# Half of the meta keys on either side of each key strip, their probabilities transposed once per four strips

## The chip, the cores and the metric

The kernel runs on one core of a Trainium2 chip. The metric is the time of one execution on the device in microseconds (us), as the median of several runs. The engines are named as in the profile: PE is TensorE's matrix multiplication, PEld its loading of weights, DVE is VectorE, ACT is ScalarE, POOL is GpSimd, SP is SyncE, which here only issues DMAs.

## The reference, cut to what matters

One layer of an encoder trunk: a combined input projection, a neighbourhood attention over a grid of 16 rows and 64 columns (1024 tokens), a gated linear recurrence, a gated merge, a feed-forward block. The change touches the attention alone. Each of 1024 tokens attends, in each of 8 heads of 64 dimensions, to the tokens of a window of 8 rows and 16 columns around it, and always to 16 learned meta keys; one softmax runs over both.

```
s_win  = einsum(q, k_window) * scale          # + bias, -1e30 outside of the window
s_meta = einsum('bhrcd,bmhd->bhrcm', q, k_meta) * scale       # 16 per token
p      = softmax(concat([s_win, s_meta]))
o      = einsum(p_win, v_window) + einsum('bhrcm,bmhd->brchd', p_meta, v_meta)
```

## The kernel before, in words

**Tiling.** A strip is 8 of the 64 grid columns in all 16 rows, that is 128 tokens; there are 8 strips. A query strip `s` needs the key strips `s-1`, `s` and `s+1` (strips 0 and 7 have two). Heads are worked on in pairs: the loop `for p in range(NPAIR)` (L547) makes four passes, and in each of them the two heads `i` stand on partitions 0 to 63 and 64 to 127 of the projections.

**Numbers in two parts.** Products of fp32 precision are made from a high part (a rounded copy, written by ACT) and a low part (the rest, a DVE subtraction); the helper `split` (L95) does both. `KS`/`KL` hold the high and low parts of the keys, `QX` those of the queries on the two halves of the partitions, `V` the high part in its first 64 columns and the low part in the second 64.

**The keys.** `KS` and `KL` are laid out as 8 strips of `SW = 144` columns: 128 keys of the strip and then all 16 meta keys (L531, L577 to L581). The scores of strip `s` are one product over the neighbouring strips, 432 columns (288 at both ends), so the 16 meta keys come three times in it; the mask `NB` (built from `wmask` on the host, and the bias) lets only those of the centre strip count.

**`scores(s, i)`** (L605): two matmuls (L612, L613), a DVE operation that adds the mask and takes the row's minimum (L618), ACT's exponential with the row sum (L620), the reciprocal and the multiplication by it on DVE (L621, L622). The result is a tile `pr` of 432 columns, five buffers.

**`values(s, i)`** (L625): the probabilities are transposed in blocks of 128 columns on PE, one per key strip (L633) and a fourth one for the centre's meta columns (L635), which takes the 16 meta columns and the 112 before them. All go into one PSUM bank of the tag `t` (two banks) and are split into `PH` and `PL` by ACT (L644) and DVE (L645). Every fourth strip, a group, the products with the values follow into one bank `ov`: one over 512 columns with the meta values in `V[:, 8]` (zero in the rows that aren't meta) for the high parts (L649), two for each of five key strips (L656 high parts, L657 low parts), and one over 512 columns for the low parts of the meta keys (L658). DVE then adds both halves of `ov` into `OT` (L660, L662).

There are 16 steps `(s, i)` in a pass, and the values of a step come two steps behind its scores. A pass has four groups, the kernel 16.

**What sets the order.** The framework's planner draws up the order of each engine's instructions at build time from the dependencies and from the order of the program, as a static list for each engine. It mixes the projections of the next pass (L135 to L137, three matmuls for each of 8 blocks) among the attention of this one; in the last pass the first gate products (L691 to L693) take that part. `block_sums` (L600) makes POOL build sums for a later stage, and POOL adds the bias to the mask (L555). `KS`, `KL`, `QX`, `V` and `NB` have one buffer each, so those of the next pass wait for this one's last reader.

## Time and profile before

| | |
|---|---|
| median of 3 runs | 1551.93 us (1550.94 to 1554.89) |
| the profiled execution | 1550.2 us, its span 1548.4 us |
| PE busy | 1502.1 us, 97% of the span |
| PEld busy | 1253.5 us, 81% |
| DVE busy | 1008.4 us, 65% |
| ACT busy | 654.7 us, 42% |
| POOL busy | 401.8 us, 26% |
| mean granted TensorE clock | 0.998 |

Busy is the share of the span in which an engine worked on at least one instruction. Matmuls overlap, so the duration of a single one is longer than the distance to the next one's start; where a cost on PE is meant, it is the distance between starts that counts.

### The profile page before, as it was taken

The numbers are of one execution on the slowest core, as the hardware profiler recorded it, in microseconds if no ns is written. First come the engines' busy times: TensorE is split into PE (matmuls) and PEld (weight loads), VectorE is DVE, ScalarE is ACT, GpSimd is POOL, SyncE is SP. The second block draws the span as 40 slices with busy tenths as digits, with TensorE's granted clock in tenths as the row PEclk, the third lists the DMA queues.
The fourth block names the chain that finished last, engine by engine and source line by source line (L and its number), as shares of the span: only waits on it lengthen the run. The fifth ranks groups of instructions, "written<-read, shape, count | busy, mean of one in ns | idle before, by whom it ended". The sixth has DMA issues, their size and how long they took to land.

```text
span 1548.4 us, 23448 instructions
## 1 busy us (share of the span) xinstructions
PE 1502.1 (97%) x9188; PEld 1253.5 (81%) x9188; DVE 1008.4 (65%) x1592; ACT 654.7 (42%) x1168; POOL 401.8 (26%) x359
## 2 busy tenths in 40 slices
PE   6999999999999998999999999999999999999998
PEld 5788888878888887888888887888888788887886
DVE  6666666664876877666475369666666444879566
ACT  6231313124665666334122245555555433434444
POOL 4413131315315310011000032444444200237033
PEclk9999999999999999999999999999999999999999
DMA  5101010113123128434951324444444576563224
GB/s 181 43 28 56 28 56 28 55 29 128 49 72 119 55 69 272 136 123 163 339 178 41 109 91 148 165 155 153 153 150 148 169 273 233 190 231 107 98 82 150
DMA packets 142335, 195.61 MB, mean 126 GB/s; under 512 B 8064, under 2 KB 90112, under 8 KB 142224
## 3 DMA queue, kind: packets, MB, share of 16 engines
q1 hardware_dynamic: 133856, 173.40, 33.8%
q10 hardware_dynamic: 6192, 13.37, 2.2%
q0 software_dynamic: 2176, 7.34, 1.3%
q8 instruction: 72, 1.18, 0.3%
q14 instruction: 39, 0.32, 0.1%
HBM read 139.55 MB, written 54.53 MB: 125 GB/s over the span
## 4 chain that ended last, share of the span: by engine, by line
PE 83%; DVE 9%; issue 3%; ACT 2%; DMA 2%; POOL 1%; DVEq 0%; POOLq 0%; SPq 0%; ACTq 0%
PE mm L135 11%; PE mm L136 10%; PE mm L137 10%; PE mm L1112 4%; PE pa L1112 4%; PE pb L691 4%; PE pb L692 4%; PE pb L693 4%; PE pc L1112 4%; PE pb L1112 4%; PE pc L693 2%; PE pc L692 2%; PE pc L691 2%; PE pa L692 2%; PE pa L691 2%
## 5 line engine op out<-in xcount | busy, mean ns | idle before, releaser
L135 PE MATMUL mm<-aT,hi 128*128 128x512 f32 (+2 forms) x640 | 230.2, 360 | 2.7 <-DVE QX L563 1.5
L137 PE MATMUL mm<-aT,lo 128*128 128x512 f32 (+2 forms) x640 | 227.8, 356 | 0.0
L136 PE MATMUL mm<-aT,hi 128*128 128x512 f32 (+2 forms) x640 | 226.6, 354 | 0.0
L97 DVE TENSOR_TENSOR dl<-ur,dh 128x1024 fp32r<-128x1024 f32 x55 | 76.6, 1393 | 93.7 <-ACT dh L96 93.5
L135 PEld LDWEIGHTS mm<-aT,hi 128*128 128x128 f32 x640 | 121.9, 191 | 17.2 <-issue 1.7
L137 PEld LDWEIGHTS mm<-aT,lo 128*128 128x128 f32 x640 | 121.8, 190 | 13.5 <-POOL lo L126 0.3
L136 PEld LDWEIGHTS mm<-aT,hi 128*128 128x128 f32 x640 | 121.9, 190 | 12.4
L96 ACT CAST dh<-ur 128x1024 fp32r<-128x1024 f32 x55 | 57.9, 1053 | 162.5 <-issue 78.1
L125 ACT CAST hi<-raw 128x1024 fp32r<-128x1024 f32 x36 | 37.8, 1051 | 106.7 <-PE mm L136 75.6
L974 ACT CAST wh<-sx 128x512 fp32r<-128x512 f32 x70 | 42.5, 618 | 94.7 <-DMA sx<-in_w_up 33.1
L975 DVE TENSOR_TENSOR wl<-sx,wh 128x512 fp32r<-128x512 f32 x70 | 51.2, 738 | 31.0 <-ACT wh L974 31.0
L975 DVE TENSOR_TENSOR wl<-raw,wh 128x512 fp32r<-128x512 f32 x46 | 50.2, 1090 | 23.7 <-ACT wh L974 22.9
L979 ACT ACTIVATE uv<-uv 128x512 f32<-128x512 f32 x48 | 30.4, 632 | 67.4 <-DVE uv L1090 50.0
L1095 POOL TENSOR_TENSOR us<-u,uv 128x512 f32<-128x512 f32 x15 | 24.0, 1603 | 133.4 <-ACT uv L980 133.4
L1202 POOL TENSOR_TENSOR w<-w,tt 128x512 f32<-128x512 f32 x16 | 23.3, 1458 | 134.0 <-DVE tt L1201 120.4
L399 POOL TENSOR_TENSOR Y<-X,TN 128x512 f32<-128x512 f32 x20 | 35.0, 1749 | 86.1 <-DVE X L396 86.1
L691 PE MATMUL pb<-nt,wh 128*128 128x512 f32 x128 | 50.4, 394 | 3.6 <-DVE uv L1083 2.6
L126 DVE TENSOR_TENSOR lo<-raw,hi 128x1024 fp32r<-128x1024 f32 x34 | 43.2, 1270 | 15.6 <-ACT hi L125 15.4
L92 POOL TENSOR_SCALAR rtm<-ssq 128x1 f32<-128x1 f32 (+1 forms) x17 | 6.4, 376 | 180.4 <-ACT junk L924 156.0
L618 DVE CUSTOM_DVE_ANT_0 pr<-nsc,NB 128x432 f32<-128x432 f32 (+1 forms) x64 | 35.2, 559 | 26.6 <-PE nsc L613 26.5
L1112 PE MATMUL mm<-dl,dh 128*128 128x512 f32 x126 | 49.9, 396 | 2.1 <-DVE dl L97 2.1
L135 PE MATMUL mm<-o,hi 128*128 128x512 f32 x128 | 50.0, 390 | 0.6 <-DVE mix L850 0.6
(380 smaller groups left out, 4409.3 us busy)
## 6 DMA issues: line engine op xcount, KB each, us to landing
raw<-in_w_in SPq DMA_DIRECT2D x56, 512.0 KB, 3.9
ur<-usp SPq DMA_DIRECT2D x55, 512.0 KB, 3.5
raw<-in_w_up SPq DMA_DIRECT2D x16, 1024.0 KB, 5.5
usp<-us SPq DMA_DIRECT2D x60, 256.0 KB, 2.0
sg<-gsp SPq DMA_DIRECT2D x16, 512.0 KB, 4.3
w<-in_w_dn SPq DMA_DIRECT2D x16, 512.0 KB, 4.5
usp<-uv SPq DMA_DIRECT2D x30, 256.0 KB, 2.2
gsp<-gv ACTq DMA_DIRECT2D x24, 256.0 KB, 2.4
```

The lines of the kernel that those rows point to most:

```text
L96: act.copy(hi, src)
L97: dve.tensor_tensor(lo, src, hi.bitcast(F32), op=ALU.subtract)
L126: eng.tensor_tensor(lo[:, :kc], raw[:, :kc], hi[:, :kc].bitcast(F32), op=ALU.subtract)
L135: pe.matmul(ps, lh, rh, start=first, stop=False)
L136: pe.matmul(ps, lh, rl, start=False, stop=False)
L137: pe.matmul(ps, ll, rh, start=False, stop=last)
L691: pe.matmul(ps, lhs[0][:, c], rhs[0][:, k], start=first and k == 0, stop=False, skip_group_check=True)
L692: pe.matmul(ps, lhs[0][:, c], rhs[1][:, k], start=False, stop=False, skip_group_check=True)
L693: pe.matmul(ps, lhs[1][:, c], rhs[0][:, k], start=False, stop=k == 3, skip_group_check=True)
L974: act.copy(v(hi), src)
L975: dve.tensor_tensor(v(lo), src, v(hi).bitcast(F32), op=ALU.subtract)
L1112: pe.matmul(ps, a[n == 2][:, q, j * P:(j + 1) * P], b[n == 1][:, q], start=first and n == 0, stop=last and n == 2, skip_group_check=True)
```

## The change

The meta keys are split into two halves of 8. The key tile becomes one row of 10 blocks of 136 columns, `[8 meta, 128 keys, 8 meta, 128 keys, ...]`, the halves taking turns. The scores of a middle strip are cut out so that the centre's keys have 8 meta keys on either side: 128 + 8 + 128 + 8 + 128 = 400 columns, each meta key once; at both ends 272 columns. Four strips write into one tile `pr` (two buffers). After the fourth, one DVE copy gathers the meta columns of all four into a tile `pm` of 64 columns. `values` transposes three blocks for a strip (two at the ends), and once in a group `pm`; from this, ACT writes the high parts to partitions 0 to 63 of `PM` and DVE the low parts to partitions 64 to 127. The two products over 512 columns are replaced by four over 128 columns, one per strip, with a weight tile `VM` each, in which the meta values stand in that strip's 16 rows twice (against the high and against the low parts). `VM` is made in each pass by four POOL multiplications with a small mask `mmask`, loaded once. A separate transpose and split for the meta values replaces the ninth block of `V`; the meta values are copied by three ACT instructions in place of one.

```
-SW = P + NM
+SW = P + NM // 2
+KO = NM // 2
+KW = 10 * SW
...
-        KS = [npl.tile([P, 8, SW], F32R, name=f"KS{i}") for i in range(2)]
+        KS = [npl.tile([P, KW], F32R, name=f"KS{i}") for i in range(2)]
...
-        V = npr.tile([P, 9, 2, P], F32R, name="Vn")
+        V = npr.tile([P, 8, 2, P], F32R, name="Vn")
+        VM = npr.tile([P, 2, 4, P], F32R, name="VM")
+        mm_sb = npr.tile([P, 2, 4], F32, name="mm_sb")
+        sp.dma_start(mm_sb.rearrange("p a b -> p (a b)"), mmask)
...
             def mev_vn(ps):
-                act.copy(vT[:, 8, P - NM:], ps)
+                v8 = vT[:, 8].rearrange("p (a c) -> p a c", c=2 * NM)
+                for o, m, n in ((0, 0, NM), (NM, KO, KO), (NM + KO, 0, KO)):
+                    act.copy(v8[:, :, o:o + n], ps[:, m:m + n].unsqueeze(1).broadcast_to([P, 4, n]))
...
+            pt = bank("t", "vmt")
+            pe.transpose(pt[:, 0], vT[:, 8], ident)
+            vh = npr.tile([P, P], F32R, tag="vh", name="vh")
+            vl = npr.tile([P, P], F32, tag="vl", name="vl")
+            split(vh, vl, pt[:, 0])
+            for q, v in enumerate((vh.bitcast(F32), vl)):
+                for i in range(2):
+                    pool.tensor_tensor(VM[:, i, :, 64 * q:64 * q + 64],
+                                       v[:, 64 * i:64 * i + 64].unsqueeze(1).broadcast_to([P, 4, 64]),
+                                       mm_sb[:, q].unsqueeze(2).broadcast_to([P, 4, 64]), op=ALU.mult)
...
             def scores(s, i):
-                w = len(js) * SW
+                e = s % 4
+                if e == 0:
+                    po["pr"] = npr.tile([P, 4, 2 * SW + P], F32, tag="pr", name="pr", bufs=2)
+                k0, c0, w, o = ((0, P, 2 * SW, 408) if s == 0 else
+                                (KO + (s - 1) * SW, 0, 2 * SW, 688) if s == 7 else
+                                (KO + (s - 1) * SW, 0, 2 * SW + P, 0))
+                pe.matmul(sc[:, :w], QX[i][:, s], KS[i][:, k0:k0 + w], start=True, stop=False)
+                pe.matmul(sc[:, :w], QX[i][:, s], KL[i][:, k0:k0 + w], start=False, stop=True)
+                prw = pr[:, e, c0:c0 + w]
...
+                if e == 3:
+                    po["pm", i] = npr.tile([P, 8 * KO], F32, tag="pm", name="pm", bufs=2)
+                    dve.tensor_copy(po["pm", i].rearrange("p (e h c) -> p e h c", h=2, c=KO),
+                                    pr[:, :, P:P + 2 * SW].rearrange("p e (h c) -> p e h c", c=SW)[:, :, :, :KO])
...
             def values(s, i, pr):
-                for k in range(m):
-                    pe.transpose(pt[:, k], pr[:, k * SW:k * SW + P], ident)
-                pe.transpose(pt[:, m], pr[:, cen * SW + NM:cen * SW + NM + P], ident)
+                for a in range(a0, a1):
+                    pe.transpose(pt[:, a], pr[:, e, a * SW:a * SW + P], ident)
+                split(PH[:, 3 * e + a0:3 * e + a1], PL[:, 3 * e + a0:3 * e + a1], pt[:, a0:a1])
                 if e < 3:
                     return
+                PM = npr.tile([P, P], F32R, tag="PM", name="PM", bufs=2)
+                pt = bank("t", "pmt")
+                pe.transpose(pt[:64, 0], po["pm", i], ident)
+                act.copy(PM[:64], pt[:64, 0])
+                dve.tensor_tensor(PM[64:], pt[:64, 0], PM[:64].bitcast(F32), op=ALU.subtract)
                 ov = bank("b", "pov")
-                pe.matmul(ov, V[:, 8, i], PH[:, 9:22:4], start=True, stop=False)
                 for a in range(-1, 5):
...
-                pe.matmul(ov, V[:, 8, i], PL[:, 9:22:4], start=False, stop=True)
+                for q in range(4):
+                    pe.matmul(ov[:, q], VM[:, i, q], PM, start=False, stop=q == 3, skip_group_check=True)
```

## Rows read from the trace of the kernel before

**Rows 1.** The page, busy time of each engine, share of the span, instructions.
```profile
PE 1502.1 (97%) x9188; PEld 1253.5 (81%) x9188; DVE 1008.4 (65%) x1592; ACT 654.7 (42%) x1168; POOL 401.8 (26%) x359
```

**Rows 2.** Windows, attention of first and last pass: PE, PEld, DVE, ACT, POOL busy.
```profile
381.00:417.00 36.00, 35.56 (x218) 29.33 (x217) 33.83 (x96) 26.89 (x64) 5.04 (x5) 1.00 0.15 48
...
553.00:592.00 39.00, 36.54 (x208) 29.79 (x207) 35.08 (x96) 32.15 (x70) 0.00 (x0) 1.00 0.33 105
```

**Rows 3.** Waits, 350 to 600 us: who waited for whom, us, times, longest.
```profile
PE ppt L633 <- DVE PT L645: 2.4, 1, 2.4
PEld pov L649 <- ACT PT L644: 2.3, 9, 0.5
...
PE ppt L633 <- DVE pr L622: 1.4, 3, 0.5
```

**Rows 4.** Timeline of PE, 387 to 420 us: start, us, instruction; a step's transposes.
```profile
390.16 0.49 PE L633 MATMUL ppt<-ident,pr 128*128 128x128 f32 x3
390.48 0.27 PE L635 MATMUL ppt<-ident,pr 128*128 128x128 f32 x1
390.51 0.47 PE L136 MATMUL mm<-aT,hi 128*128 128x512 f32 x1
390.82 0.39 PE L137 MATMUL mm<-aT,lo 128*128 128x512 f32 x1
```

**Rows 5.** Groups by line and shape, 350 to 600 us: busy us, mean ns.
```profile
L645 DVE TENSOR_TENSOR PT<-ppt,PT 128x512 fp32r<-128x512 f32 x48 | 32.4, 677 | 0.4
...
L613 PE MATMUL nsc<-KL,QX 128*128 128x432 f32 x48 | 17.2, 358 | 0.0
...
L555 POOL TENSOR_TENSOR NB<-NB,bs 128x256 f32<-128x256 f32 x16 | 11.6, 749 | 0.0
...
L621 DVE RECIPROCAL rc<-sm 128x1 f32<-128x1 f32 x64 | 9.5, 154 | 2.3 <-ACT pr L620 2.2
...
L613 PE MATMUL nsc<-KL,QX 128*128 128x288 f32 x16 | 4.7, 296 | 0.0
...
L645 DVE TENSOR_TENSOR PT<-ppt,PT 128x384 fp32r<-128x384 f32 x8 | 4.5, 558 | 0.2
...
L645 DVE TENSOR_TENSOR PT<-ppt,PT 128x256 fp32r<-128x256 f32 x8 | 3.3, 410 | 0.0
...
L581 DVE TENSOR_TENSOR KL<-mm,KS 64x128 fp32r<-64x128 f32 x8 | 2.3, 288 | 5.2 <-ACT KS L580 5.2
```

**Rows 6.** Timeline of PE, 387 to 420 us: a group's products, weights of 128 or 64 columns.
```profile
408.24 0.47 PE L649 MATMUL pov<-PT,Vn 128*128 128x512 f32 x1
408.55 0.22 PE L656 MATMUL pov<-PT,Vn 128*128 128x128 f32 x1
408.60 0.23 PE L657 MATMUL pov<-PT,Vn 128*64 128x128 f32 x1
408.67 0.33 PE L656 MATMUL pov<-PT,Vn 128*128 128x256 f32 x1
408.84 0.28 PE L657 MATMUL pov<-PT,Vn 128*64 128x256 f32 x1
...
409.88 0.39 PE L658 MATMUL pov<-PT,Vn 128*128 128x512 f32 x1
410.11 0.49 PE L633 MATMUL ppt<-ident,pr 128*128 128x128 f32 x3
```

**Rows 7.** Timeline of PE, the same stretch: the next pass's key projection begins.
```profile
411.45 0.28 PE L135 MATMUL mm<-aT,hi 128*128 128x256 f32 x1
411.57 0.28 PE L136 MATMUL mm<-aT,hi 128*128 128x256 f32 x1
```

**Rows 8.** Timeline of DVE, 381 to 420 us: one multiplication alone, one beside POOL.
```profile
405.09 0.36 DVE L622 TENSOR_SCALAR pr<-pr,rc 128x288 f32<-128x288 f32 x1
...
413.25 1.02 DVE L622 TENSOR_SCALAR pr<-pr,rc 128x288 f32<-128x288 f32 x1
```

**Rows 9.** Timeline of POOL, 374 to 445 us; in brackets its idle time before.
```profile
413.10 2.46 POOL L555 TENSOR_TENSOR NB<-NB,bs 128x384 f32<-128x384 f32 x3 [30.16 <-DMA NB<-in_wmask]
```

More of the change, by code (lines that the diff above doesn't have):

```diff
@@ L49, in layer @@
 def layer(ctx: ExitStack, tc: tile.TileContext, x, meta, w_in, w_na, w_hg, w_o, w_up, w_dn,
-          g_mix, g_mlp, g_fin, gain, bias, lbl, lmask, wmask, out):
+          g_mix, g_mlp, g_fin, gain, bias, lbl, lmask, wmask, mmask, out):
     nc = tc.nc
@@ L568, in ev_k @@
                     b = 64 * i
-                    hi = strips(KS[i], b, t0, n)
+                    hi = strips(key_strips(KS[i]), b, t0, n)
                     act.copy(hi, grid(ps, b))
-                    act.copy(strips(KS[i], 64 - b, t0, n), grid(ps, b))
-                    dve.tensor_tensor(strips(KL[i], b, t0, n), grid(ps, b), hi.bitcast(F32), op=ALU.subtract)
+                    act.copy(strips(key_strips(KS[i]), 64 - b, t0, n), grid(ps, b))
+                    dve.tensor_tensor(strips(key_strips(KL[i]), b, t0, n), grid(ps, b), hi.bitcast(F32),
+                                      op=ALU.subtract)
             def mev_k(ps):
@@ L626, in values @@
+                return pr
+            def values(s, i, pr):
                 g, e = divmod(s, 4)
                 if e == 0:
-                    po[i] = [npr.tile([P, 22, P], F32R, tag=f"PT{q}", name=f"PT{q}") for q in range(2)]
+                    po[i] = [npr.tile([P, 12, P], F32R, tag=f"PT{q}", name=f"PT{q}") for q in range(2)]
                 PH, PL = po[i]
-                m = len(js)
+                a0, a1 = (1, 3) if s == 0 else (0, 2) if s == 7 else (0, 3)
                 pt = bank("t", "ppt")
-                for k in range(m):
-                    pe.transpose(pt[:, k], pr[:, k * SW:k * SW + P], ident)
@@ L667, in layer @@
             for st in steps:
-                pend.append((*st, *scores(*st)))
+                pend.append((*st, scores(*st)))
                 if len(pend) > 2:
```

83 lines of the change are left out of this document (35 added, 48 removed).

## The prediction

> **What bounds the kernel now.** I began with the page's busy times [rows 1]: PE is busy in 97% of the span, no other engine in more than 65%. That alone could mislead, since overlapping matmuls look busy however they are spaced, so the second view was the table by windows over the attention [rows 2]. There PE works in 35.56 of 36 us in the first pass, and DVE in 33.83 of the same 36: in this stage two engines are full at once, and a saving on one is worth no more than the other lets through. ACT has a quarter of the stretch to itself, POOL nearly all of it. Third, the waits [rows 3]: in 250 us PE itself waits for DVE at the transposes for 2.4 + 1.4 = 3.8 us and for hardly anything else. So DVE is full but seldom late, because the planner has put projection matmuls of the next pass between the steps. The limit is PE's own work, with DVE close behind.
>
> It has to be seen whether that cover runs out. The attention's scores of the first pass are through by 408 us, yet the next pass's key projection, the last matmuls for which there are free PSUM banks before its queries can be evacuated, starts only at 411.45 us [rows 7]: 24 matmuls 0.12 us apart, 2.9 us of cover, are left over. That decides how I read every saving below: PE's counts as long as DVE doesn't become later by more than those 2.9 us in a pass, relative to PE.
>
> **The change, part by part.** I count in distances between starts on PE, and in durations on DVE, over all four passes.
>
> *Transposes.* In a step of four, the starts run from 390.16 to 390.82 us with one 512-column matmul inside [rows 4]; such a matmul takes 0.23 us (409.88 to 410.11, [rows 6]), so a transpose costs (0.66 - 0.23)/4 = 0.108 us. Before, a pass has 12 middle strips with four and four end strips with three, 60; after, 12 x 3 + 4 x 2 = 44 and one for each group, 48. Over four passes 48 fall away: **-5.2 us**. The ninth value block is transposed once before and once after.
>
> *Scores.* From 432 to 288 columns L613 becomes 358 - 296 = 62 ns shorter [rows 5], 0.43 ns a column. 32 columns less in 48 x 2 middle matmuls give 1.3 us, 16 less in 16 x 2 end ones 0.2 us: **-1.5 us**.
>
> *Values.* In each of 16 groups L649 (0.31 us to the next start) and L658 (0.23 us) go, 0.54 us [rows 6]; four products over 128 columns come, each with its own weights of 128 columns. No run of four such stands in the trace. A 128-column matmul followed by weights of 64 columns gives way after 0.06 us (408.55 to 408.60, rounded): 0.24 us for four is the lower end. Where full weights follow a 128-column matmul, the 256-column L656 takes 0.17 us (408.67 to 408.84) rather than the 0.12 us of the same width in a stream [rows 6, 7], so a full load costs some 0.06 us more than it can hide: 0.12 us each, 0.48 us for four. Four times 0.17 us, 0.68 us, is the upper end. The four new loads all are of that kind, so I take 0.48 us: 0.06 us saved a group, **-1.0 us**; the ends are -4.8 and +2.2 us. The ten matmuls between stay; their operand is only stored in another order.
>
> PE's sum is -7.7 us.
>
> *DVE.* A split of 384 in place of 512 columns saves 677 - 558 = 119 ns in 48 steps, 5.7 us; 256 in place of 384 saves 148 ns in 8, 1.2 us [rows 5]. The last strip's split in two instructions becomes one, some 0.29 us (the price of a 128-column subtraction, L581) in 8 steps, 2.3 us. The shorter mask addition, at the 0.93 ns a column of those splits, saves 30 ns in 48 steps and 15 ns in 16, 1.7 us. New are 16 subtractions into `PM`, 64x128 like L581, 0.288 us each, 4.6 us, and 16 copies of 64 columns into `pm`: above 0.154 us (L621, a single column) and below 0.288 us, I take 0.2 us, 3.2 us. Net -3.1 us, between -1.7 and -3.9 us. This doesn't stand on the path and enters the sum at nothing: it is 0.8 us a pass against PE's 1.9 us, so DVE falls behind PE by 1.1 us a pass, which the 2.9 us of cover takes up [rows 7]. With the cover gone it would cost those 1.1 us a pass.
>
> *ACT.* It copies a quarter less in each split and gains a 64x128 copy a group and two small copies a pass for the meta values. With a quarter of the stretch idle [rows 2] I put this at nothing; behind each new copy the next step's exponential is queued, and were it all seen it would be a 64x128 operation a group, 16 x 0.29 = 4.6 us, less the copies' own saving.
>
> *The new chain at the end of a group.* The gather of `pm` waits on DVE behind the fourth strip's multiplication, then come the transpose, ACT's copy, DVE's subtraction, and only then the four last products; the transpose also needs a turn of one of the two `t` banks. Beside it run the ten matmuls from 408.55 to 409.88 us, 1.33 us [rows 6]. On the other side the old first product L649 waited for the last strip's split, 2.3 us in 9 groups on the loading of weights [rows 3]; the new first one needs only the early strips. I set both against each other at nothing; the bounds are a gain of 2.3 us and the first rival.
>
> *POOL.* Four multiplications of 128x256 a pass, each like L555 of that size, 0.749 us [rows 5], 3.0 us. POOL was idle for 30.16 us in that stretch [rows 9], so its own time costs nothing; queued behind them are `block_sums` and the next pass's mask, which waited for their DMA anyway. What they do to DVE does count: beside POOL's additions at 413.10 us a DVE multiplication over 288 columns took 1.02 us in place of 0.36 us, 0.66 us more [rows 8, 9]. In 3.0 us one or two such multiplications (16 in some 36 us of a pass) meet POOL, so up to 1 us a pass, 4 us in all; half an operation's wait on average, and some of it covered, leaves **+1.2 us** (0 to 4).
> The Trainium skill speaks against the change here: its page "SBUF — State Buffer", section "Who interferes with whom", says that a DVE operation in a two-port mode and a GpSimd operation share one pair of ports and whoever comes second waits for the whole instruction. By that, the trace's 0.66 us agrees (most of one 0.749 us operation), and a multiplication that comes just too late pays it in full; the third rival takes this at its full price.
>
> *Small things.* One more DMA of a few bytes on SP, before the mask and bias loads, which have the length of a projection to land; memory clearing of `KL` 18% wider on POOL: nothing, each at most one issue or one operation under 1 us, once.
>
> **Sum**: -7.7 + 1.2 = -6.5 us. The profiled execution took 1550.2 us (span 1548.4 us), so 1543.7 us by its clock; the median of the runs is 1.7 us above it, 1551.93 us, and that is what is predicted against: **1545.4 us**, -0.4%. What a measurement can tell from no change is about 0.3%, 4.7 us. The likeliest case's own range is 1540.4 us (values at their best end, no contention: -11.5 us) to 1549 us (values at nothing saved, contention 4 us: -2.7 us).
>
> **The rivals.**
> *The chain is late* (slower). If, at the end of a group, DVE has one step's split (0.677 us) ahead of the new subtraction (0.288 us) and PE stands before the four products for that long, 0.97 us a group, 15.4 us come on top of -7.7: +7.7 us, 1559.6 us. It decides above 7.7/16 = 0.48 us exposed a group. For it: DVE is full in this stretch [rows 2], and the old L649 did wait in 9 of 16 groups [rows 3]. Against it: 1.33 us of matmuls run beside the chain, and the planner can put projection matmuls in between. 13%.
> *DVE becomes the bound* (no change). If the cover is less than I read, each pass ends when DVE does, and only DVE's -3.1 us are gained: 1548.8 us. For it: DVE's 94% [rows 2] and the 3.8 us for which PE waits for it already [rows 3]. Against it: the leftover of 2.9 us [rows 7]. 16%.
> *POOL holds up DVE at full price* (no change). If each of the 16 multiplications on POOL delays one on DVE by 0.66 us, and PE follows it in its fixed order, 10.6 us against 7.7: +2.9 us, 1554.8 us; at half of that, 1549.5 us. For it: [rows 8]. Against it: DVE reads PSUM in most of its work, and its multiplications are 16 of 96 instructions in the stretch [rows 2]. 13%.
> That fewer transposes or columns are issued than written is excluded by the code. What stays open is the planner: a new list for each engine can shift waits by a microsecond or two either way, in the last pass too, where PE's one long wait of 2.4 us lies [rows 3].
>
> **Chances.** Forecast 58%, all of it faster by over 0.3%; DVE and POOL together 29%, within 0.3%; the late chain 13%, slower by over 0.3%. The range of 1538.5 to 1554 us holds the forecast with its ends, 2 us of the planner's below, the DVE case and POOL's up to nearly its full price; the late chain is left out.
>
> **What would show it.** Right: 192 transposes in L633's place at 0.11 us, the four new products at about 0.12 us apart, the attention windows shorter by nearly 2 us a pass with PE as full as now. Wrong: waits of PE before the new products or for `PM` (the chain); more PE waits for DVE at the transposes, and multiplications on DVE of 1 us beside POOL in the first 10 us of a pass (POOL); PE idle with DVE full at the ends of passes (DVE). A time at 1552 us or above with no such waits in the attention would mean that the gain was given back in a later stage.

## The result, and the profile after

The changed kernel is slower: 1555.95 us (median of 20 runs, 1553.50 to 1559.07) beside 1551.31 us for the kernel before in the same session, a ratio of 1.003 with a 95% interval of 1.0022 to 1.0038. A repetition of both in a later session gave 1.0025 (1.0012 to 1.0037), and the kernel before against itself 1.0003 (0.9991 to 1.0016). The forecast was 1545.4 us, faster. The profiled execution after took 1557.05 us, its span 1555.2 us.

The page hides the difference: every engine is about as busy as in [rows 1].

```profile
PE 1502.0 (97%) x9172; PEld 1249.5 (80%) x9172; DVE 1005.9 (65%) x1616; ACT 647.5 (42%) x1182; POOL 409.9 (26%) x374
```

The windows show it. Columns: stretch, its length, then busy us (instructions) of PE, PEld, DVE, ACT, POOL, granted clock, DMA share, GB/s. The first and the last row answer to [rows 2]; between them stands the second pass, cut at its last score (466.6 us) and its last product (476.7 us), with the stretch up to the next pass's first score. The two rows on 965 to 975 us are for the last section.

```profile
381.00:417.00 36.00, 34.19 (x204) 27.63 (x202) 32.63 (x98) 24.60 (x62) 7.06 (x8) 1.00 0.19 61
...
440.40:466.60 26.20, 25.15 (x147) 20.23 (x147) 24.62 (x80) 17.95 (x49) 2.58 (x4) 1.00 0.07 21
466.60:476.70 10.10, 9.37 (x62) 7.74 (x60) 9.85 (x24) 5.95 (x15) 4.25 (x4) 1.00 0.30 100
476.70:498.00 21.30, 21.30 (x134) 19.37 (x134) 7.40 (x13) 9.54 (x25) 14.92 (x16) 1.00 0.44 142
...
965.00:970.00 5.00, 2.45 (x11) 1.69 (x10) 4.97 (x7) 0.62 (x1) 0.87 (x1) 0.96 0.41 157
970.00:975.00 5.00, 5.00 (x17) 3.78 (x16) 2.04 (x4) 1.88 (x3) 1.86 (x2) 0.70 0.81 261
...
553.00:592.00 39.00, 38.14 (x217) 30.74 (x216) 34.48 (x104) 28.24 (x69) 2.58 (x4) 1.00 0.32 97
```

The same three stretches in the kernel before:

```profile
437.70:463.90 26.20, 26.17 (x154) 21.55 (x153) 24.67 (x74) 18.70 (x46) 1.29 (x1) 1.00 0.07 21
463.90:474.70 10.80, 10.20 (x73) 8.91 (x72) 10.30 (x23) 7.69 (x18) 4.86 (x5) 1.00 0.29 98
474.70:495.30 20.60, 19.98 (x120) 17.84 (x120) 8.54 (x13) 8.15 (x20) 14.53 (x15) 1.00 0.46 148
```

Read DVE first: 24.67 us of 26.20 before, 24.62 us of 26.20 after. The 16 strips take the same 26.2 us, though PE has less to do. PE was full there (26.17 us) and now idles for a microsecond. The whole pass is 36.3 instead of 37.0 us long; that is near what DVE lost (0.5 us: 34.97 to 34.47), not what PE lost. One pair of readings is not much for so small a step: in the repetition of the kernel before (r_before, below) this pass takes 36.3 us too, and over the first three passes and both profiles of each kernel the mean falls from 36.8 to 36.4 us. The stretch behind the pass, in which DVE works for 8 us of 20, grew from 20.6 to 21.3 us; the mean of the three such stretches, again over both profiles, from 20.1 to 21.2 us.

Next the projection matmuls that lie in the passes; here the windows count those of the line of the first of three products (hi times hi), so the number of all is three times the x. Before, then after, for the first three passes:

```profile
381.20:418.30 37.10, 9.38 (x26) 4.92 (x26) 1.00 0.14 45
437.70:474.70 37.00, 9.19 (x25) 4.72 (x25) 1.00 0.14 43
495.30:532.00 36.70, 9.16 (x25) 4.74 (x25) 1.00 0.14 44
```
```profile
382.50:419.50 37.00, 8.50 (x22) 4.19 (x22) 1.00 0.18 58
440.40:476.70 36.30, 7.96 (x21) 3.96 (x21) 1.00 0.14 43
498.00:534.20 36.20, 7.96 (x21) 3.97 (x21) 1.00 0.14 43
```

PE had more room in a pass and was given less to put into it: about 64, 61 and 61 projection matmuls instead of 77, 74 and 74. What isn't done there is done between the passes, where PE is busy throughout: hence the 21.3 us.

The waits from 350 to 600 us (who waited for whom: us, times, longest), answering to [rows 3]:

```profile
PE pov L682 <- DVE OT L691: 2.9, 8, 0.7
...
PE pmt L672 <- DVE PT L99: 2.1, 3, 0.8
...
DVE low L689 <- PE pov L687: 0.5, 2, 0.2
```

PE now waits in two places that didn't exist: a group's first product (L682) waits until DVE has emptied the one bank `ov` of the group before (L691), and the meta transpose (L672) waits for a `t` bank that DVE's split still reads. DVE in turn hardly waits for PE at the group's end any more, for 0.5 us in place of 3.3: before, its copy of the group's low half waited for the last product,

```profile
DVE low L660 <- PE pov L658: 3.3, 6, 1.6
```

and most of that little slack is gone. In the timeline of PE (start, us, instruction, idle time and releaser in brackets) the two waits and, in the middle, the four new products look like this; the last line is from the stage behind the attention:

```profile
398.91 0.36 PE L682 MATMUL pov<-PT,Vn 128*128 128x256 f32 x1 [0.57 <-DVE OT L691]
...
402.71 0.61 PE L687 MATMUL pov<-PM,VM 128*128 128x128 f32 x4
403.16 0.84 PE L666 MATMUL ppt<-ident,pr 128*128 128x128 f32 x6
...
417.87 0.30 PE L672 MATMUL pmt<-ident,pm 128*64 128x128 f32 x1 [0.80 <-DVE PT L99]
...
603.97 0.50 PE L720 MATMUL mm<-aT,hi 128*128 128x512 f32 x1 [0.88 <-ACT go L741]
```

From the starts of all matmuls in the trace I worked out a balance. "Attention" runs from the first score to the first of the last 4167 matmuls, those of the later stages, which stand in the same order in most kernels here (in six runs the first few are mixed with the attention's last); the "seam" is the next 117 of them (the first gate products). "Columns" is the sum of the matmuls' columns at 2.4 GHz (fp32 transposes at twice that time); a "wait" is a distance between two starts that exceeds the columns by over 0.15 us; what is left, small excesses, are the "short losses". The two profiles of each kernel stand beside each other:

| | attention | columns | short losses | waits | seam |
|---|---|---|---|---|---|
| before | 212.9 / 213.6 | 184.9 | 20.5 / 20.2 | 7.6 / 8.5 | 29.1 / 28.2 |
| after | 212.5 / 212.2 | 174.8 | 23.3 / 23.4 | 14.3 / 14.0 | 30.7 / 32.2 |

Ten microseconds of columns went; 3 came back as short losses, 6 as waits; the attention is 0.9 us shorter on the mean. That is a sum of two unlike parts. The first three passes, with the stretches behind them, are 2.1 us longer (170.7 to 172.8 us on the mean of the two profiles); the last pass, in which the kernel before has its longest wait of PE for DVE (2.4 us in [rows 3], 3.0 us in the repetition) and the changed kernel has none like it, is 3.0 us shorter.

The seam is 2.8 us longer, and that turns the sign. There ACT's list has put the split of a block sum ahead of a gate's work, and it waits for its DMA (start, us, instruction):

```profile
601.85 0.62 ACT L98 CAST at<-gv 128x512 fp32r<-128x512 f32 x1 [2.85 <-DMA gv<-tsp_t]
...
603.33 0.59 ACT L741 ACTIVATE go<-mm 128x512 f32<-128x512 f32 x1
```

PE's gate product at 603.97 us waits for 0.88 us until that sigmoid (L741) has emptied its bank. With the smaller gaps around it that is 1.3 us of the 2.8, in both profiles of the changed kernel and in neither of the kernel before. The rest isn't that list's alone. A later wait for the split of the weights (1.6 and 0.7 us before, 1.7 us in both after) gives some 0.6 us, and the seam of the repetition r_after holds a stretch in which the granted clock fell:

```profile
610.00:615.00 5.00, 4.47 (x12) 3.27 (x13) 3.58 (x4) 2.36 (x4) 0.00 (x0) 0.66 0.74 213
```

So does the attention of r_before (0.68 from 590 to 595 us); there eight products of 512 columns start 0.44 instead of 0.23 us apart, so by estimate each such fall cost 1.6 us. Without the two the attention would be level (0.1 us shorter) and the seam 2.0 us longer. Either way the sum is some 2 us, at the lower end of the repetition's interval and short of the first measurement's 4.6 us. The two profiles of one kernel differ by up to 5 us in their spans, so the rest isn't located. It doesn't show behind the seam: from there to the end the kernel before takes 925.2 us in its first profile and 929.3 us in its repetition, the changed kernel 929.5 us in both.

### The profile page after: what moved, and what is told of

Same layout as the page of the kernel before. It is cut to its first block, busy times and chain, and to the rows that moved or that the text cites. A ratio compares the mean times of both kernels' runs of the same rounds, so it can differ in the third digit from the quotient of the medians.

```text
span 1555.2 us, 23488 instructions
## 1 busy us (share of the span) xinstructions
PE 1502.0 (97%) x9172; PEld 1249.5 (80%) x9172; DVE 1005.9 (65%) x1616; ACT 647.5 (42%) x1182; POOL 409.9 (26%) x374
## 4 chain that ended last, share of the span: by engine, by line
PE 76%; DVE 12%; issue 4%; ACT 4%; DMA 3%; POOL 1%; SPq 0%; DVEq 0%; POOLq 0%; ACTq 0%
PE mm L137 10%; PE mm L138 9%; PE mm L139 9%; PE mm L1141 4%; PE pa L1141 4%; PE pb L720 4%; PE pb L722 4%; PE pb L721 4%; PE pc L1141 4%; PE pb L1141 4%; PE pc L720 2%; PE pc L722 2%; PE pc L721 2%; PE pa L720 2%; PE pa L721 2%
## 5 line engine op out<-in xcount | busy, mean ns | idle before, releaser
L1003 ACT CAST wh<-sx 128x512 fp32r<-128x512 f32 x70 | 42.5, 618 | 94.9 <-DMA sx<-in_w_up 31.9
L1231 POOL TENSOR_TENSOR w<-w,tt 128x512 f32<-128x512 f32 x16 | 23.3, 1459 | 134.0 <-DVE tt L1230 116.4
L646 DVE CUSTOM_DVE_ANT_0 pr<-nsc,NB 128x400 f32<-128x400 f32 (+1 forms) x64 | 33.3, 529 | 26.8 <-PE nsc L640 26.5
```

Source lines behind the costliest of these rows:

```text
L1003: act.copy(v(hi), src)
```

## The experiments

All ratios are against the kernel before, timed on the same chip in the same five rounds, with the 95% interval.

**Controls (r_before, r_after).** Nothing edited.

> The kernel before, unchanged, for a second trace of it. Theory A (the change's loss lies in the attention alone, later differences of the two first traces are chance): the gaps behind the attention vary between the two traces of before by as much as 2 to 5 us. Theory B (the later stages lose systematically): this trace shows the same late gaps as the first of before, within 1 us: 1.0 us at the first waits of the mix stage, full clock at 945 to 975 us. Ratio 1.000 within 0.002.

> The changed kernel, unchanged, for a second trace of it. Attention from the first score to the last product takes again about 212.6 us (theory: static order, its waits repeat to a few tenths). Theory A: the later 5 us of the first trace (1.6 us at 602 us, 2.6 us at 749 us, the clock at 969 us) come and go. Theory B: they are there again. Ratio 1.003.

Measured: 1.0003 (0.9991 to 1.0016) and 1.0025 (1.0012 to 1.0037). The loss is real, some 4 us. Of the later differences only the one at 602 us comes back as the changed kernel's own; the wait near 750 us and the fall of the clock near 970 us stand in both profiles of the changed kernel, but in the repetition of the kernel before too. The first profile of the kernel before was the exception there.

**Reordering the end of a group (e_rev, e_same).** In e_rev the products over the key strips run backwards, so that the first one needs the last split and can't be pulled ahead:

```
-                for a in range(-1, 5):
+                for a in range(4, -2, -1):
```

> The changed kernel with the key strips of a group's products taken from the last to the first, so that the first product needs the last strip's split, as the meta product did before; work the same. Theory 1 (the first products became ready early, the planner put them ahead on PE, where they stand waiting for the bank and the splits): the 5.3 us of long gaps before these products fall below 2 us and the attention becomes 3 to 5 us shorter, ratio to before 0.998 to 1.001. Theory 2 (the additional turn of the transposed meta block through the two banks is what costs): no change, gaps before the meta transposes stay 2.6 us, ratio 1.003.

In e_same the meta transpose uses the free quarter of the last strip's bank instead of a turn of its own:

```
-                pt = bank("t", "pmt")
-                pe.transpose(pt[:64, 0], po["pm", i], ident)
+                pe.transpose(pt[:64, 3], po["pm", i], ident)
```

> The changed kernel with the transposed meta block written into the free fourth part of the bank that the group's last strip uses, so that it takes no turn of its own; order of products as in the changed kernel. Theory 2: gaps before the meta transposes (2.6 us) go and those of the next strip shrink, attention 2 to 4 us shorter, ratio 0.999 to 1.001. Theory 1: the gaps before the key strips' products stay above 4 us, time within 1.5 us of the changed kernel.

Measured: 1.0022 (1.0012 to 1.0033) and 1.0027 (1.0011 to 1.0042); the attention 214.2 us in both, with 16.5 and 15.3 us of waits. Each edit took away most of the wait that it was aimed at (before the products over the key strips 5.3 us became 2.5, before the meta transposes 2.6 became 0.4), and the time appeared in front of other instructions (in e_rev 11.5 of the 16.5 us stand in front of the strips' transposes, against 4.6 us of 14.3 in the changed kernel). Neither wait is a cause by itself. e_same came out as theory 1 had said for it, e_rev as neither theory.

**Is PE's work worth time at all? (b_nolow, a_dummy.)** b_nolow is the kernel before without the product for the low parts of the meta keys' probabilities (L658), 16 products of 512 columns:

```
-                pe.matmul(ov, V[:, 8, i], PL[:, 9:22:4], start=False, stop=True)
```

> The kernel before without the 512-column product of the meta keys' low probabilities (left out; the high part stays), so 16 x 0.23 = 3.7 us of work less on PE and nothing changed on DVE and ACT. Theory P (PE's work bounds the attention, as forecast): -3.7 us, ratio 0.9976, same number of projection matmuls within the attention or more. Theory D (the attention is as long as its chain over DVE and ACT takes, and PE waits for what it no longer has to do): 0 to -1 us, ratio 0.9995 to 1.000, and the long gaps on PE grow by 3 us.

a_dummy is the changed kernel with 48 unread transposes added, a fourth one for each middle strip:

```
+                if 0 < s < 7:
+                    pe.transpose(pt[:, 3], pr[:, e, SW:SW + P], ident)
```

> The changed kernel with a fourth transpose, which nobody reads, in each of the 48 middle strips: 5.2 us more work on PE, as before the change, DVE and ACT as changed. Theory P: +5 us against the changed kernel, ratio to before 1.006. Theory D: 0 to +1 us, ratio 1.002 to 1.004, the long gaps shrink by 4 us or more.

Measured: 0.9978 (0.9967 to 0.9989) and 1.0046 (1.0030 to 1.0062). Before the change 3.5 us of columns fewer made the attention 5.4 us shorter, with 6.4 us of waits; after it 5.1 us more made it 5.3 us longer. In time b_nolow met theory P's number, while a_dummy lies between the two theories. So PE's work does cost time, which is what the forecast assumed; but b_nolow also cuts DVE's waiting for the last product (3.3 to 1.8 us), and its passes hold 80 projection matmuls instead of 74.

Where a_dummy's time lies says more. Its second pass up to the last score, beside the 26.20 us of the changed kernel:

```profile
441.50:467.80 26.30, 25.14 (x153) 20.43 (x152) 24.92 (x80) 17.84 (x49) 2.58 (x4) 1.00 0.07 21
```

A pass has 1.3 us of transposes more, and the strips take as long as without them, with PE as busy and idle for a microsecond as before: the new list has four projection matmuls (0.9 us) fewer among the strips and 18 fewer in the pass (43 instead of 61), and the stretch behind it takes 24.9 us instead of 21.3. The time that the strips take looks given, and what doesn't fit into it is done later.

**Relieving VectorE (b_nonorm, a_nonorm).** Both kernels without the reciprocal and the multiplication of the softmax:

```
-                dve.reciprocal(rc, sm)
-                dve.tensor_scalar(prw, prw, rc, None, op0=ALU.mult)
```

> The kernel before without the reciprocal and the multiplication by it (the probabilities stay unnormalised), so 64 x some 0.5 us less on DVE, 8 us a pass, and nothing changed on PE. Theory P: PE was waiting for 6 us in all, so at most -2 to -4 us, ratio 0.9975 to 0.999. Theory D: the chain gets shorter, the gaps on PE go, -5 to -6 us, ratio 0.996.

> The changed kernel without the reciprocal and the multiplication, otherwise as above. Theory D: with DVE's part made shorter PE bounds again, and now the 9.9 us less work on PE come through: -8 to -12 us against the changed kernel, 5 to 9 us faster than the same kernel before, ratio to before 0.991 to 0.995. Theory P with waits made by the new order alone: those waits stay, -2 to -4 us against the changed kernel, not faster than the kernel before with the same left out.

Measured: 0.9967 (0.9957 to 0.9978) and 0.9978 (0.9968 to 0.9989). The waits of PE fall by 6 to 7.5 us in both (to 1.6 and 6.8 us), so they hang on VectorE. a_nonorm's second pass up to the last score:

```profile
436.80:456.20 19.40, 19.16 (x121) 15.97 (x120) 16.75 (x50) 16.21 (x46) 2.33 (x4) 1.00 0.10 28
```

With 8 us less on DVE the 16 strips take 19.4 instead of 26.2 us, and PE hardly idles any more (14 projection matmuls fewer lie among them, 3.0 us of the 6.8); in b_nonorm they take 23.3 us. So VectorE did set the pace of the changed kernel's strips. Yet the changed kernel doesn't get ahead in time, and theory D's 0.991 to 0.995 for it missed: its attention, 206.1 us, is only 1.4 us shorter than the other's, and its seam is 31.3 us against 28.6.

**Ending the groups later (a_def3, b_def3).** A group's end (meta transpose, products, sum) is written three strips later in the program, in both kernels; in the changed one that puts 97 projection matmuls into a pass:

```
-                if len(pend) > 2:
-                    values(*pend.pop(0))
+                    late.append(values(*pend.pop(0)))
+                    if len(late) > 3:
+                        (late.pop(0) or (lambda: None))()
```

> The changed kernel, with the end of each group (transposing the meta probabilities, the group's products, the sum of the halves) written three strips later in the program, so that three more strips' scores and transposes stand ahead of it; nothing else. In the order of TensorE this puts 97 projection matmuls between the first score and the last product of a pair, where the changed kernel has 64, 61, 61 (and 78 in place of 52 in the last pair). Theory A (the columns taken from TensorE are saved, and are lost again as waits, because its static order puts the products, the meta transpose and the transposes of the next strips ahead of what they wait for): the long waits of TensorE in the attention fall from 14.4 us to some 8, the attention from 212.2 us to 206 to 208, and the time against the kernel before from 1.0025-1.003 to 0.998-1.000. Theory B (VectorE paces the strips of a pass, and what TensorE saves beside it can't be used): the attention stays at 211 to 213 us, the waits stay as long and only change place, as in the two reorderings run so far, ratio 1.002-1.004.

> The kernel before with the same edit, as the control: the end of each group written three strips later; 80 projection matmuls in a pair's pass where the kernel before has 77, 74, 74. Theory A: before has little wait to lose (7.6 us in the whole attention), ratio 0.998-1.001; the deferral then narrows the distance between the two kernels by some 4 us. Theory B: the deferral does the same to both, whatever that is, and the changed kernel stays 3 to 5 us behind.

Measured: 1.0012 (1.0001 to 1.0022) and 1.0010 (1.0000 to 1.0020). The two kernels are level, as theory A had it, but not for its reason: the attention is 213.8 us against 212.1, and the waits (14.8 us) have only moved to the strips' transposes, behind VectorE's split:

```profile
PEld ppt L666 <- DVE PT L99: 11.6, 14, 1.9
PE ppt L666 <- DVE PT L99: 8.0, 13, 1.5
```

Theory A, that the order alone loses the time, finds no support in a third reordering that leaves the attention no shorter; it isn't excluded, since 1.0012 lies between what the two theories gave, and the 2 us or so that the kernel gained in time stand in no stage of its one profile.

**A second bank for the products (a_b2, b_b2).**

```
-    psum_pools(mx=1, s=2, t=2, b=1)
+    psum_pools(s=2, t=2, b=2)
```

> The changed kernel with two PSUM banks for the groups' products in place of one, and two for the projections in place of three. Theory A': the wait for the single bank of the products is the one that counts (TensorE waited 2.9 us at it in 8 places, and the products behind it were spread): the attention falls by 3 to 5 us, ratio 0.999-1.001. Theory B: no less than 1.002. Rival: with one bank less for projections TensorE waits for their evictions in its place, 1.004 or more.

> The kernel before with the same banks (two for the products, two for the projections), as the control: its products wait for nothing in the trace, so that the second bank can't help by itself. Theory A': 1.000-1.003, so that the changed kernel with two banks is level with it or ahead. Theory B: the same edit moves both kernels alike and the distance of 3 to 5 us stays.

Measured: 1.0125 (1.0109 to 1.0141) and 1.0081 (1.0065 to 1.0097). The rival was right: PE no longer waits for L691, but for evictions, in a_b2

```profile
PE mm L137 <- DVE QX L577: 6.0, 3, 2.1
```

where the changed kernel has none in the same stretch (its one such wait, 1.5 us, lies ahead of the attention). The third projection bank is worth more than the second product bank. It also shows that projection matmuls in a pass are no gain in themselves: there are 91 in these passes, which last 43 us.

**Loading VectorE (b_dve, a_dve).** One unread copy of 128 columns per strip, in both kernels:

```
+                dve.tensor_copy(npr.tile([P, P], F32, tag="junk", name="junk"), prw[:, :P])
```

> The kernel before with one more VectorE instruction per strip, behind the normalisation: a copy of the strip's first 128 probabilities into a tile that nothing reads (64 copies of 128 columns; by the changed kernel's copy of 64 meta probabilities, 0.18 us, some 0.2 us each, 3.2 us per pair, 12.8 us in all). Theory D (VectorE is full from a pair's first score to its last product and sets the length of that pass, whatever TensorE has to do in it): the passes of 36.6 to 37.1 us become about 40, the last score comes 3 us later than at +26.2, and the kernel is 5 to 11 us slower (1.003-1.007; less than the sum because more projection matmuls, 83 to 99, lie in the longer pass). The forecast's view (TensorE bounds, VectorE has cover): not over 2 us, 0.999-1.001.

> The same unread copy per strip in the changed kernel (75, 64, 64, 68 projection matmuls in the passes instead of 64, 61, 61, 52). Theory D: passes of 36.2 us become about 39.4, 4 to 10 us slower than the changed kernel, ratio to before 1.005-1.009. The forecast's view, with some 10 us of columns less on TensorE than before: VectorE has all the more cover, level with the changed kernel, 1.002-1.004.

Measured: 1.0054 (1.0034 to 1.0075) and 1.0075 (1.0058 to 1.0092), that is 8 us more than the kernel before and 7 to 8 us more than the changed one. The copies were dearer than I had estimated, in b_dve

```profile
L623 DVE COPY junk<-pr 128x128 f32<-128x128 f32 x64 | 16.3, 254 | 0.4
```

and half of it shows in the time; the longer passes also take up more projection matmuls (83 instead of 74 in the second pass of b_dve). The second pass of b_dve, then of a_dve, up to the last score:

```profile
438.20:465.80 27.60, 27.45 (x159) 22.55 (x158) 26.18 (x86) 19.18 (x46) 0.00 (x0) 1.00 0.07 20
```
```profile
439.10:467.20 28.10, 26.30 (x152) 20.67 (x151) 26.18 (x91) 17.73 (x49) 2.75 (x5) 1.00 0.07 20
```

DVE is busy for 95 and 93% of the stretch, as it was without the copies (94%), and the stretch is 1.4 and 1.9 us longer; the pass up to the last product went from 37.0 to 39.4 us and from 36.3 to 37.9. So load on VectorE costs time in both kernels. More than that the two runs don't decide. The 2 us at most that I had set for the forecast's view rested on copies of 0.2 us, 3.2 us a pass; at the 0.254 us measured they are 4.1 us a pass, and of those the forecast's own cover of 2.9 us would have let 1.2 us through, 4.7 us in four passes (an estimate), and some 9 us in the changed kernel, which had 1.1 us less cover left. Nor is b_dve's time located: its profiled execution, 1553.1 us, is the shortest of its six (median 1559.9 us), and the attention in it is 216.1 us, 2.9 us above the mean of the kernel before. In a_dve it is 222.4 us, 10 us more than in the changed kernel, 9 of them waits.

**Moving work from VectorE to ScalarE (a_h2d3, b_h2d3).** Groups' ends three strips later, and every second multiplication on ACT:

```
+                if s % 2:
+                    act.activation(prw, prw, AF.Copy, scale=rc)
+                else:
                     dve.tensor_scalar(prw, prw, rc, None, op0=ALU.mult)
```

> The changed kernel with the groups' ends three strips later (as in the run before of that edit) and the normalisation of every second strip on ScalarE instead of VectorE (32 of 64 multiplications of 0.42 us, 3.4 us of VectorE's work per pair). 88 projection matmuls in a pass. Theory D: what VectorE no longer has to do comes off the pass: the deferred kernel's 40.4 us become about 37 us with 15.5 us of projections in them, the attention falls from 213.8 to 202-207 us, ratio 0.995-0.998. If TensorE's order and not VectorE's work holds the pass: as the deferred kernel alone, 1.000-1.002. If ScalarE, 85% busy in the first 23 us of the pass, takes VectorE's place: 1.001 or more.

> The kernel before with the same two edits, as the control (74 projection matmuls in a pass, as in the kernel before). Theory D: VectorE relieved, TensorE's work bounds the kernel before again: its attention falls by 2 to 5 us (as without the normalisation, where it fell by 6), ratio 0.997-0.999, and the changed kernel with the same edits is now 1 to 5 us ahead of it, since only there TensorE has 10 us of columns less. If the columns saved are worth nothing in any case: the two are level.

Measured: 0.9999 (0.9985 to 1.0013) and 1.0042 (1.0028 to 1.0055). The changed kernel comes out some 6 us ahead of the other with the same edits, a little more than expected, but both ratios missed what theory D gave for them (0.995 to 0.998 and 0.997 to 0.999). What the second edit did is read against the runs with the first alone: from a_def3 to a_h2d3 the attention falls from 213.8 to 211.7 us, from b_def3 to b_h2d3 it rises from 212.1 to 216.6 us. Second pass up to the last score, a_h2d3, then b_h2d3 (22.5 and 26.4 us in a_def3 and b_def3):

```profile
440.20:462.00 21.80, 21.41 (x126) 17.43 (x125) 19.82 (x68) 19.15 (x51) 2.45 (x4) 1.00 0.09 26
```
```profile
438.00:464.20 26.20, 26.16 (x154) 21.07 (x153) 23.87 (x70) 21.58 (x52) 0.64 (x1) 1.00 0.07 21
```

In b_h2d3 DVE works less (23.87 us instead of 24.67) and ACT more (21.58 instead of 18.70), and the 26.2 us stay; PE is full there, and its loading of weights now waits for the multiplication on ACT:

```profile
PEld ppt L636 <- ACT pr L623: 3.0, 7, 0.6
```

So a multiplication moved to the other engine is no relief by itself. That the changed kernel gains from it fits its smaller load on ACT (a quarter less to copy in each split), but no run separates that.

**VectorE relieved and projections kept in the passes (a_nn3, b_nn3).** The normalisation left out and the groups' ends three strips later, in both:

> The changed kernel without the normalisation (its reciprocal and multiplication are left out, as in the earlier pair of runs, so that the probabilities are not divided by their sums) and with the groups' ends three strips later: VectorE relieved and 90 projection matmuls kept in a pass (36 to 38 without the deferral). If both are needed for the columns saved on TensorE to come through: the attention falls below the 207.3 us of the kernel before without the normalisation, to 200-204 us, ratio 0.993-0.996. If TensorE loses in waits what it saves whatever the order and whatever VectorE does: 205-208 us of attention, 0.997-0.999.

> The kernel before with the same two edits (normalisation left out, groups' ends three strips later), as the control: 58 projection matmuls in a pass. By either theory as without the deferral, since its waits are short there (losses of 22.7 us beside 184.9 us of columns): attention 206-208 us, ratio 0.996-0.998. If the columns come through, the changed kernel is 2 to 7 us ahead of this one; if not, level or behind.

Measured: 0.9979 (0.9964 to 0.9994) and 1.0019 (1.0005 to 1.0033). In time the changed kernel is 4 to 6 us ahead; in the trace the columns still don't come through. The attention is 207.7 us against 208.3, where I expected 200 to 204: waits 7.3 against 2.6 us, short losses 25.6 against 20.9. The second passes up to the last score, a_nn3, then b_nn3:

```profile
436.80:457.30 20.50, 20.50 (x124) 16.81 (x123) 16.02 (x47) 15.91 (x44) 2.32 (x4) 1.00 0.09 27
```
```profile
434.70:458.30 23.60, 23.60 (x142) 19.59 (x141) 18.96 (x47) 18.89 (x46) 0.17 (x1) 1.00 0.08 23
```

With VectorE relieved (78 and 80% busy) PE is full in both and the stretch is 3.1 us shorter in the changed kernel with about as many projection matmuls in it (29 and 32 by the lists), as one expects of a stage that PE bounds; behind the last score a_nn3 gives it back, in a tail that takes 17.7 us against 10.5 with the projections that lie there. The distance in time comes rather from the seam, 28.4 us against 31.1, where now b_nn3, a form of the kernel before, has the wait for the sigmoid:

```profile
PE mm L695 <- ACT go L716: 0.9, 1, 0.9
```

So that part of the seam's loss belongs to a list that happened to be drawn up, and can strike either version. Over the attention the seven pairs give (changed kernel minus the other, in us):

| pair | ratios | attention | columns | waits + short losses |
|---|---|---|---|---|
| as they are (means) | 1.0025 / 1.0003 | -0.9 | -10.1 | +9.1 |
| def3 | 1.0012 / 1.0010 | +1.7 | -9.3 | +10.9 |
| b2 | 1.0125 / 1.0081 | +6.9 | -10.0 | +17.0 |
| dve | 1.0075 / 1.0054 | +6.3 | -10.5 | +16.7 |
| h2d3 | 0.9999 / 1.0042 | -4.9 | -9.9 | +5.0 |
| nonorm | 0.9978 / 0.9967 | -1.4 | -10.1 | +8.6 |
| nn3 | 0.9979 / 1.0019 | -0.6 | -10.1 | +9.4 |

The saving of columns is there in all of them and at most half of it ever reaches the attention's length. No full version beat the kernel before; a_h2d3 equals it. Faster than both is b_nolow, which does without the low parts of the meta probabilities.

## Why the prediction was wrong, step by step

*PE's terms were right.* Transposes: 48 fewer, -5.1 us of columns for -5.2 forecast. Scores: -1.5 for -1.5. Values: from 402.71 to 403.16 us a group's four products take 0.45 us, forecast 0.48. With the 3 us by which the short losses grew (the new products have 2.8 us between them: 0.11 us from one to the next, where 128 columns alone are 0.05 us), PE's work fell by some 7 us, forecast 7.7. One bound was set wrongly, to no effect on the range: the likeliest case's upper end of 1549 us takes the values at nothing saved, while their own upper end of +2.2 us would have given 1551.4 us.

*DVE's terms were right in the sum, in part by luck.* By-form groups of the changed kernel from 350 to 600 us (busy us, mean ns), answering to [rows 5]:

```profile
L99 DVE TENSOR_TENSOR PT<-ppt,PT 128x384 fp32r<-128x384 f32 x48 | 26.1, 548 | 0.9 <-ACT PT L98 0.3
...
L650 DVE TENSOR_SCALAR pr<-pr,rc 128x400 f32<-128x400 f32 x48 | 21.7, 453 | 0.2
...
L99 DVE TENSOR_TENSOR PT<-ppt,PT 128x256 fp32r<-128x256 f32 x16 | 6.6, 415 | 0.0
...
L622 POOL TENSOR_TENSOR VM<-vl,mm_sb 128x256 fp32r<-128x256 f32 x8 | 5.7, 727 | 0.0
...
L653 DVE COPY pm<-pr 128x64 f32<-128x64 f32 x16 | 4.9, 309 | 0.1
...
L674 DVE TENSOR_TENSOR PM<-pmt,PM 64x128 fp32r<-64x128 f32 x16 | 4.5, 284 | 0.5
```

The splits fell from 42.5 to 32.7 us, mask additions and multiplications by 2.7, and 9.4 us came new: -3.1 us, as forecast. But the `pm` copies cost 0.31 us each instead of 0.2, 1.7 us more in all, and that was made up for by the splits (0.6 us more saved than forecast) and by the shorter multiplications (1.0 us), which the forecast had left out.

*The step that failed is the one before them: "That decides how I read every saving below: PE's counts as long as DVE doesn't become later by more than those 2.9 us in a pass".* The condition held: PE's work fell by some 7 us and DVE's by 3.1, so that DVE fell behind by about 1 us a pass. The conclusion didn't: in place of 7.7 us the attention lost 0.9, and PE's waits grew by 6. What was wrong is the cover. I took the 24 matmuls at the end of the first pass [rows 7] for leftover work that lets PE's saving through, and so read a stage with two full engines [rows 2] as PE's. They were in use already. In the kernel before, the chain that ended last runs over DVE at this place (start, us, engine, tile and line), and PE stands waiting for it with 15 of the 24 matmuls done:

```profile
410.31 0.69 DVE low L660
...
413.32 0.96 DVE pr L622
```
```profile
414.41 0.41 PE L633 MATMUL ppt<-ident,pr 128*128 128x128 f32 x2 [0.44 <-DVE pr L622]
```

The three waits of PE for L622 in [rows 3], which I had passed over, are the ends of the first three passes.

What the runs showed in its place: in the changed kernel VectorE sets the length of the 16 strips. They take 26.2 us as before while PE idles for one of them; 1.3 us of transposes more pushed projections out of them and left them at 26.3 us (a_dummy), and 8 us less for DVE brought them to 19.4 us (a_nonorm). PE's saving there became room, and the new list put no projections into it but took 13 matmuls out of a pass, so that the stretches between the passes grew by 1.1 us and the passes shrank by 0.4. Of the rival "DVE becomes the bound" (1548.8 us, 16%) that is the mechanism, but not the gain of 3.1 us that it promised.

That VectorE alone costs the saving is not shown. With it relieved (nonorm and nn3) the changed kernel's attention is ahead by only 1.4 and 0.6 us; and projections kept in the passes (88 to 97 in def3, h2d3 and nn3) didn't bring the columns through either.

*"I set both against each other at nothing" (the end of a group).* The first product no longer needs the last split, as I wrote, but for that very reason the planner put it far ahead, in front of an `ov` bank that wasn't empty; and the meta transpose waits for its bank. Together 5 us of PE's waits here. That they aren't a cost of their own, e_rev and e_same showed: the waits are where PE's idle time comes to lie. The rival "the chain is late" named this place and the wrong mechanism.

*POOL.* The four multiplications took 0.63 and 0.73 us on the mean, as estimated (0.75). Their toll on DVE can be read off the timelines of DVE and POOL: one multiplication beside them takes 0.42 us, the next 0.74 us.

```profile
390.46 0.42 DVE L650 TENSOR_SCALAR pr<-pr,rc 128x400 f32<-128x400 f32 x1
...
391.41 0.74 DVE L650 TENSOR_SCALAR pr<-pr,rc 128x400 f32<-128x400 f32 x1
```
```profile
390.56 1.36 POOL L622 TENSOR_TENSOR VM<-vl,mm_sb 128x256 fp32r<-128x256 f32 x2
```

In each profile of the changed kernel five multiplications of DVE beside them took 0.56 to 0.78 us, 1.5 us more in all than the usual 0.42 to 0.44 us each; the forecast had 1.2 us. DVE's splits (0.41 and 0.55 us) and mask additions (0.42 and 0.56 us) beside them were no longer than elsewhere. What of the 1.5 us reached the time isn't separated.

*The planner, "a microsecond or two either way", was no small term.* The wait for the sigmoid in the seam, 1.3 us, is its doing, and so are the matmuls that left the passes; the pairs above, in which the same change is worth between -5 and +7 us of attention, differ in their lists as well as in their work. No run changes the work and keeps the list, so its share isn't measured.

What stays open: with VectorE relieved, the changed kernel's PE still has some 5 us more waits and 3.3 to 4.7 us more short losses than the other (nonorm and nn3). Some 3 us of the short losses are the new products', which the forecast had priced. Of the waits the trace names VectorE's split of a strip as the one waited for (PE 2.1 us and its loading of weights 5.3 us in a_nonorm), although VectorE is busy for only 86% of the strips' stretch; a third `t` bank, so that the next strip's transposes need not wait for the split, was not tried. And some 2 us of the measured loss lie in no stage that two profiles agree on.

## What to carry to other kernels

Where two engines are full in the same stretch, find out which one sets its length before pricing a saving on the other: follow the chain that ended last through the stretch, then put useless instructions on each engine in turn and look in the trace whether the stretch gets longer, with a load that the rival view could not cover. Work removed from the engine that is full only because filler was scheduled beside it is worth no more than the filler that comes in its place. And with an order drawn up by a planner, any edit redraws it as far as the next stage; compare several pairs of the same two versions before saying what the edit itself does.

## What the runs showed of the hardware

The granted clock fell for some microseconds far behind the change, and in the repetitions nearer to it (r_before's last pass, r_after's seam). In the changed kernel PE is busy for 2.45 of 5 us from 965 us on, waiting, and in the next 5 us it is granted 0.70 of its clock, a mean over a part at 2.4 and a part at 1.2 GHz, and issues 17 matmuls (the rows above). The repetition of the kernel before has the like,

```profile
970.00:975.00 5.00, 5.00 (x19) 3.83 (x17) 1.52 (x3) 0.72 (x2) 2.95 (x2) 0.79 0.68 238
```

while the profile that the forecast rested on shows 1.00 there, 24 matmuls, and gains some 1.5 us by it (7 matmuls at 0.21 us).

```profile
970.00:975.00 5.00, 5.00 (x24) 4.13 (x23) 3.01 (x4) 3.93 (x7) 3.14 (x3) 1.00 0.28 108
```

A forecast made against one profile inherits such luck.

DVE beside POOL: a 64-column copy takes 0.19 us alone and 0.72 us while POOL adds to the mask (from 413.87 us for 3.43 us).

```profile
396.95 0.19 DVE L653 COPY pm<-pr 128x64 f32<-128x64 f32 x1
...
414.96 1.75 DVE L128 TENSOR_TENSOR lo<-raw,hi 128x1024 fp32r<-128x1024 f32 x1
...
416.64 0.72 DVE L653 COPY pm<-pr 128x64 f32<-128x64 f32 x1
```

The weights' low part before it, 1.75 us, is the longest of 15 with a median of 1.23 us. Of such a copy a forecast has to take the mean of 0.31 us, not the 0.19 us that it takes alone.
